# Hybrid decoder step: where the measures of the second and third units' weights stand at the start

## The chip, the cores and the metric

The kernel runs on one core of a Trainium2 chip. The metric is the time of one execution on the device in microseconds (us). The engines are named as the profile names them: PE is TensorE (matmuls; PEld its weight loads), DVE is VectorE, ACT is ScalarE, POOL is GpSimd, SP is SyncE, whose queue issues most DMAs.

## What is computed

One inference step of a decoder with two layers, for a prompt of 2048 tokens and 8 sample sequences of 4 new tokens (32 rows). Layer 0 is a linear attention (HGRN2) and a forgetting softmax attention side by side, behind one input projection; layer 1 is a gated linear attention (GLA).

```python
def even_mixer(h, w_in, ...):           # layer 0, h = rmsnorm(x, norm_even)
    proj = h @ w_in                     # 1024 -> 4*512 + 4*512 + 4
    qa, fa, ia, ga, qb, kb, vb, gb, fb = _split(proj, ...)
    f = lb + (1.0 - lb) * sigmoid(fa)
    o_a, s_a = gated_linear_chunked(qa, 1 - f, ia, log(f), hgrn_s0)
    o_a = head_rmsnorm(o_a, hgrn_gain) * silu(ga)
    o_b = fox_attend(qb, kb, vb, log_sigmoid(fb + b_fox)) * silu(gb)
    return concatenate([o_a, o_b]) @ w_out, ...
```

The change lies in the first 80 us of layer 0: the norm of the first 1056 token rows and the first columns of `h @ w_in`.

## The kernel before, in words

A full-precision product is made of three 16-bit ones: each operand is split into a high part (16 bit) and a low part (what is left), and a product is high x high, high x low, low x high (`mm3`, lines 467 to 469). Before a weight block is split it is scaled by a power of two. The scale comes from a **measure** (the largest absolute value: four reductions on VectorE, line 292, one for each quarter of the block, and one over the four results, line 294), a product on TensorE that spreads it over the partitions (`spr_...`, line 279) and a few tiny steps on VectorE (`pow_...`, lines 281, 270, 271, 272, 302; the reciprocal in line 272 is the scale). Then the **split**: of the four quarters, two go ScalarE L348 (scale), ScalarE L349 (high part), GpSimd L350 (low part), the other two ScalarE L345 (high part) and VectorE L346 (low part).

The input projection is cut into **units** of 256 weight columns. A unit has four steps: 0 fetch (DMAs), 1 measure, 2 scale, 3 split, and then its matmuls. The units of the first half of the tokens come in the order v0, g0, qf0, qf1, Bq0, Bg0, ...; in the program's names v0's weights are `Ai`, g0's `Ag`, those of qf0 and qf1 both `Aqf`. The raw weights are `wr_...`, the split ones `w_...`, the maxima `rm_...`. v0's outputs are `pt_Av` (four pairs of 128-token tiles, 48 matmuls each) and `pS_Av` (the 32 sample rows, from `sam_Av`, a copy of their columns; the four partial sums are added in line 516 and copied to `vs` in line 807). g0's are `pf_Ag`, in three segments of 352 columns of tokens for each of two halves; each ends in a silu (lines 523 to 525).

The tokens themselves are loaded (`nx`), normalized (lines 418, 400, 402, 420), turned by TensorE in pairs of 128-token tiles (`nt`, line 431), and split into `act`: high parts on ScalarE (line 462), low parts on VectorE (line 463). The last group is the 32 sample rows. The buffers of `nt` come free with the low parts. `self.last_v` is the latest low part written down so far.

`staged` runs the units: while unit j's matmuls are written down tile by tile, it writes down steps of the next units; the list `todo` says which, as pairs (unit, step), one list behind each tile. A scheduler then sets the order in each engine's queue; each engine works through its own queue strictly in that order. `issue_after(x)` binds all instructions in its block to stand behind x. The small constants of the kernel (`more_consts`: gains, `lb`, `wgr` and `wg`, masks `mlev` by way of `mtmp`, the cleared `scT`) are bound in this way behind the last token load, the last high part and the last low part.

Of the kernel before, what the change touches and what calls it, by code (L numbers as in the profile page):

```python
# [121 lines left out]
class Kern:  # L122
# [918 lines left out]
    def staged(self, us, a, b, beside=None):  # L1041

        def step(u, n):
            if u < len(us):
                self.ready[u] = us[u][0][n]()

        for j in range(a, b):
            if j:  # L1050
                todo = [[(j + 3, 0), (j + 2, 1)], [(j + 2, 2)], [(j + 2, 3)]]
            elif beside is None:
                todo = [[(2, 0), (1, 3)], [(3, 0)], [(2, 3)]]
            else:
                todo = [[(1, 0)], [], [(2, 0)], [(1, 1), (1, 2)], [(1, 3), (3, 0), (2, 1), (2, 2), (2, 3)]]
            for n, c in enumerate(us[j][1](self.ready.pop(j))):
                for x in todo.pop(0) if todo else ():
                    step(*x)
                if beside and n in (1, 3):
                    beside(2 * j + n // 2)  # L1060
                yield c
            for t in todo:
                for x in t:
                    step(*x)
# [896 lines left out]
```

## Time and profile before

| | before |
|---|---|
| timed runs (3) | 2403.77, 2410.35, 2413.72 us; median 2410.35 |
| profiled execution | 2408.25 us, its span 2405.8 us |
| mean granted clock of TensorE | 0.987 |
| PE busy | 2296.7 us (95%) |
| DVE, ACT, POOL busy | 1418.9, 1111.1, 744.1 us (59, 46, 31%) |
| DMA | 317.25 MB, mean 132 GB/s |

The span is what the trace covers; the execution's own time is 2.45 us longer. Times in rows count from the start of the span. A granted clock of 1.00 is TensorE's higher level (2.4 GHz), 0.50 the lower one (1.2 GHz). Matmuls are pipelined: each row shows some 0.27 us for a matmul of 256 columns, while they start 0.11 us apart at the higher clock.

### The profile page before, as it was taken

Reading aid. Unit: us, or ns where it says so; the run is one execution under the profiler, and the core shown is the slowest. Engines: PE = TensorE matmul, PEld = TensorE weight load, DVE = VectorE, ACT = ScalarE, POOL = GpSimd, SP = SyncE. Lnnn points to the kernel's source line nnn. Section 1 sums busy time; section 2 is a strip of 40 time slices with the busy share of each in tenths; the row PEclk is TensorE's granted clock in tenths of the full one; section 3 lists DMA queues with packets and bytes.
Section 4 is the critical chain, followed back from the end, with each engine's and each line's share of the span. In section 5 each row is a group of like instructions: output and inputs, shape, how many; then the busy total and the mean of one; then the engine's idle time right before and its main releaser. Section 6 shows DMA issues by size and latency. Waiting matters only on the chain. (4 is left out here: it accounts for less than half of the span.)

```text
span 2405.8 us, 58659 instructions
## 1 busy us (share of the span) xinstructions
PE 2296.7 (95%) x23324; PEld 1635.3 (68%) x23324; DVE 1418.9 (59%) x3345; ACT 1111.1 (46%) x2466; POOL 744.1 (31%) x839
## 2 busy tenths in 40 slices
PE   7999999999999999999997999999999999999998
PEld 5667668854655876655445876777678766666887
DVE  7556556546764548567667363665675644557554
ACT  6434243342433127466668254535443645545333
POOL 2233223112212225144465111432452222322222
PEclk9999999999999999999999999999999999999999
DMA  6231235435431276776865532122146312114453
GB/s 181 78 87 58 85 121 160 144 108 149 144 116 59 82 223 220 259 246 208 265 195 181 163 108 59 45 76 89 50 147 194 114 37 73 43 58 159 152 190 148
DMA packets 297013, 317.25 MB, mean 132 GB/s; under 512 B 39729, under 2 KB 241010, under 8 KB 296738
## 3 DMA queue, kind: packets, MB, share of 16 engines
q1 hardware_dynamic: 295234, 308.98, 40.7%
q8 instruction: 183, 3.00, 0.5%
q0 software_dynamic: 1504, 4.52, 0.5%
q14 instruction: 92, 0.75, 0.1%
HBM read 242.31 MB, written 71.11 MB: 130 GB/s over the span
## 5 line engine op out<-in xcount | busy, mean ns | idle before, releaser
L469 PE MATMUL pt_o<-w_o,act 128*128 128x256 f16 x1024 | 281.2, 275 | 4.1 <-DVE act L1597 3.9
L467 PE MATMUL pt_o<-w_o,act 128*128 128x256 f16 x1024 | 281.5, 275 | 2.4 <-ACT sg1C L523 2.4
L468 PE MATMUL pt_o<-w_o,act 128*128 128x256 f16 x1024 | 281.2, 275 | 0.0
L467 PEld LDWEIGHTS <-act 128*128 128x128 f16 x2304 | 226.9, 98 | 37.0 <-ACT act L462 4.7
L469 PEld LDWEIGHTS <-act 128*128 128x128 f16 x2304 | 226.8, 98 | 35.2 <-DVE act L1597 5.1
L468 PEld LDWEIGHTS <-act 128*128 128x128 f16 x2304 | 227.0, 99 | 33.6 <-issue 3.7
L467 PE MATMUL pt_Cv<-w_Cv,act 128*128 128x256 f16 (+1 forms) x512 | 140.3, 275 | 1.7 <-ACT act L462 0.9
L468 PE MATMUL pt_Cv<-w_Cv,act 128*128 128x256 f16 (+1 forms) x512 | 140.0, 274 | 0.0
L469 PE MATMUL pt_Cv<-w_Cv,act 128*128 128x256 f16 (+1 forms) x512 | 139.7, 274 | 0.0
L633 POOL TENSOR_TENSOR kA<-kA,fA 128x512 f32<-128x512 f32 (+1 forms) x56 | 79.0, 1411 | 191.6 <-PE gl_A L599 141.3
L1208 ACT ACTIVATE L<-L,nm,kc 128x512 f32<-128x512 f32 (+3 forms) x160 | 118.2, 740 | 37.9 <-DVE nm L1206 33.7
L633 POOL TENSOR_TENSOR kC<-kC,fC 128x512 f32<-128x512 f32 (+1 forms) x56 | 82.0, 1465 | 151.9 <-PE gl_C L599 112.5
L1216 POOL TENSOR_SCALAR L<-L,nm 128x512 f32<-128x512 f32 (+3 forms) x160 | 98.5, 629 | 65.3 <-DVE nm L1212 24.1
L1243 ACT ACTIVATE th<-pt 128x512 f16<-128x512 f32 (+3 forms) x159 | 80.6, 526 | 61.0 <-PE pt L1236 60.2
L1244 DVE TENSOR_TENSOR tl<-pt,th 128x512 f16<-128x512 f32 (+3 forms) x159 | 94.8, 609 | 22.1 <-ACT th L1243 21.0
L1236 PE MATMUL pt<-ident,L 128*128 128x128 f32 x544 | 91.9, 280 | 6.3 <-POOL L L1216 3.2
L1236 PEld LDWEIGHTS pt<-ident,L 128*128 128x128 f32 x544 | 67.2, 144 | 35.7 <-DVE tl L1244 8.7
L1360 PEld LDWEIGHTS pkt<-ident,pgcache_fox_k 128*128 128x128 f32 x512 | 57.5, 141 | 42.6 <-issue 25.1
L1360 PE MATMUL pkt<-ident,pgcache_fox_k 128*128 128x128 f32 x512 | 74.7, 278 | 7.3 <-DVE kts L1364 5.2
L467 PE MATMUL pt_Av<-w_Ai,act 128*128 128x256 f16 x256 | 70.5, 276 | 2.5 <-ACT act L462 2.5
L467 PE MATMUL fo<-th,h_v 128*128 128x512 f16 (+3 forms) x174 | 59.4, 341 | 12.4 <-ACT th L1243 9.5
L468 PE MATMUL pt_Av<-w_Ai,act 128*128 128x256 f16 x256 | 70.4, 275 | 0.8 <-POOL w_Ai L350 0.8
(950 smaller groups left out, 6756.6 us busy)
## 6 DMA issues: line engine op xcount, KB each, us to landing
pgcache_fox_k<-in_cache_fox_k SPq DMA_DIRECT2D x128, 256.0 KB, 4.3
pgcache_fox_v<-in_cache_fox_v SPq DMA_DIRECT2D x128, 256.0 KB, 3.9
yr<-yT SPq DMA_DIRECT2D x16, 1024.0 KB, 6.1
nx<-in_x_prompt SPq DMA_DIRECT2D x16, 512.0 KB, 4.9
wr_Aqf<-in_w_in_even SPq DMA_DIRECT2D x64, 128.0 KB, 3.8
wr_o<-in_w_out_even SPq DMA_DIRECT2D x32, 256.0 KB, 4.5
wr_Cv<-in_w_in_odd SPq DMA_DIRECT2D x32, 256.0 KB, 3.9
wr_Cqk<-in_w_in_odd SPq DMA_DIRECT2D x64, 128.0 KB, 3.0
```

The lines of the kernel that those rows point to most:

```text
L467: nc.tensor.matmul(ps, lh[0], rh[0], start=first, stop=False)
L468: nc.tensor.matmul(ps, lh[0], rh[1], start=False, stop=False)
L469: return nc.tensor.matmul(ps, lh[1], rh[0], start=False, stop=last)
L633: nc.gpsimd.tensor_tensor(kv[:, :, 0], kv[:, :, 0], t1.to_broadcast([P, nb, w]), ALU.mult)
L1208: self.last_exp = nc.scalar.activation(lt[:, :w], lt[:, :w], AF.Exp, bias=nm[:, 0:1], scale=ib, accum_out=nm[:, 2 + j : 3 + j])
L1216: nc.gpsimd.tensor_scalar(lt[:, :w], lt[:, :w], nm[:, 1:2], 2.0**14, ALU.mult, ALU.mult)
L1236: nc.tensor.transpose(pt[:, w : w + P], rows[b][s // 4][0][:, (s % 4) * P : (s % 4 + 1) * P], self.ident)
L1243: nc.scalar.activation(th[:, a:w], pt[:, a:w], AF.Copy),
L1244: nc.vector.tensor_tensor(tl[:, a:w], pt[:, a:w], th[:, a:w], ALU.subtract)))
L1360: nc.tensor.transpose(pk[:, j * P : (j + 1) * P], pgs[j][:, h * P : (h + 1) * P], self.ident)
```

## The change

```diff
         def step(u, n):
             if u < len(us):
-                self.ready[u] = us[u][0][n]()
+                with ExitStack() as st:
+                    if beside and n == 1 and u < 3:
+
+                        st.enter_context(self.tc.issue_after(self.last_v.ins))
+                    self.ready[u] = us[u][0][n]()
...
-                todo = [[(1, 0)], [], [(2, 0)], [(1, 1), (1, 2)], [(1, 3), (3, 0), (2, 1), (2, 2), (2, 3)]]
+                todo = [[(1, 0)], [], [(2, 0)], [(1, 1), (1, 2), (1, 3)], [(3, 0), (2, 1), (2, 2), (2, 3)]]
```

The measures of units 1 (g0, `Ag`) and 2 (qf0, the first `Aqf`) are bound behind the latest low part. When they are written down, in the lists behind v0's fourth pair of tiles and behind its sample rows, that is the last one of the sample rows. And g0's split is written down one place earlier, behind v0's last pair of full tiles, not behind the sample rows. No instruction is added or taken away.

What it does to VectorE's queue while the first token pairs are split (the difference; `act<-nt_5_229` is the low part of the sixth of eight row blocks of the first token pair, `nt_0_264` belongs to the second pair):

```order
 L346 SCALAR_TENSOR_TENSOR w_Ai_153<-wr_Ai_134,kc,w_Ai_153 128x2x256 x2
-L292 TENSOR_REDUCE rm_Ag_648<-wr_Ag_359 128x1
 L463 SCALAR_TENSOR_TENSOR act<-nt_5_229,g_even,act 128x256
-L292 TENSOR_REDUCE rm_Ag_648<-wr_Ag_359 128x1
 L400 TENSOR_SCALAR rst_n_189<-nss_187 128x1
-L292 TENSOR_REDUCE rm_Ag_648<-wr_Ag_359 128x1
 L463 SCALAR_TENSOR_TENSOR act<-nt_6_234,g_even,act 128x256
-L292 TENSOR_REDUCE rm_Ag_648<-wr_Ag_359 128x1
+L420 TENSOR_SCALAR nx_512_184<-nx_512_184,rsr_n_191 128x1024
 L463 SCALAR_TENSOR_TENSOR act<-nt_7_239,g_even,act 128x256
-L292 TENSOR_REDUCE rm_Aqf_717<-wr_Aqf_556 128x1
 L463 SCALAR_TENSOR_TENSOR act<-nt_0_264,g_even,act 128x256
```

The four measures of Ag and the four of the first Aqf (the other three stand a few rows on) are gone from among the low parts, and the norm of a later token tile (L420) has moved up.

VectorE's queue of the change from the last low part on (`nt_7_593` is the last row block of the sample rows):

```order
L463 SCALAR_TENSOR_TENSOR act<-nt_7_593,g_even,act 128x32
L292 TENSOR_REDUCE rm_Ag_648<-wr_Ag_359 128x1 x4
L506 COPY sam_Av_673<-act 128x8x32 x2
L292 TENSOR_REDUCE rm_Aqf_717<-wr_Aqf_556 128x1 x4
L165 TENSOR_SCALAR g_hgrn<-g_hgrn 128x4
L165 TENSOR_SCALAR g_gla<-g_gla 128x8
L172 TENSOR_TENSOR lb<-lb 128x4
L191 MEMSET wgr 80x512
L213 CAST mdiag<-ident 128x128
L232 MEMSET scT_835 128x1024
L232 MEMSET scT_836 128x1024
L294 TENSOR_REDUCE rm_Ag_648<-rm_Ag_648 128x1
```

The measures now stand here, among the constants, and the sum over Ag's four (L294) stands behind the two memsets of scT. Six short rows follow (a mask cast, the sum for Aqf, two gains, two of lb), then L196 (wg), L177 (lb), and these, on to the reciprocal that gives Ag's scale (the first L272):

```order
L281 TENSOR_REDUCE pow_Ag_656<-spr_Ag_654 128x1
L292 TENSOR_REDUCE rm_Aqf_883<-wr_Aqf_708 128x1 x4
L178 RECIPROCAL lb<-lb 128x4
L270 TENSOR_SCALAR pow_Ag_656<-pow_Ag_656 128x1
L210 CAST mlev_789<-mtmp 128x64
L210 CAST mlev_795<-mtmp 128x64
L516 TENSOR_TENSOR few_Av_701<-few_Av_701,pS_Av_676 32x256
L281 TENSOR_REDUCE pow_Aqf_725<-spr_Aqf_723 128x1
L294 TENSOR_REDUCE rm_Aqf_883<-rm_Aqf_883 128x1
L179 TENSOR_TENSOR lb<-lb 128x4
L271 TENSOR_SCALAR kc<-pow_Ag_656 128x1
L516 TENSOR_TENSOR few_Av_701<-few_Av_701,pS_Av_676 32x256
```

Behind these come L270 for Aqf, L184 (lb) and the L272. Before, the steps L281 to L302 of Ag stood among the low parts of the sample rows, around the measures of the second Aqf (`rm_Aqf_883`, whose place behind L281 of Ag is kept).

TensorE's queue of the change at the end of v0 (`nt_7_593` is the last transposition of the sample rows):

```order
L467 MATMUL pt_Av_597<-w_Ai_153,act 128x256
L431 MATMUL nt_7_593<-ident,nx_1024_364 128x32
L468 LDWEIGHTS act
L468 MATMUL pt_Av_597<-w_Ai_153,act 128x256
L469 LDWEIGHTS act
L469 MATMUL pt_Av_597<-w_Ai_153,act 128x256
L279 MATMUL spr_Ag_654<-ident,rm_Ag_648 128x128
L511 LDWEIGHTS sam_Av_673
L511 MATMUL pS_Av_676<-w_Ai_153,sam_Av_673 32x256
```

The product for Ag's scale (`spr_Ag`) now stands behind v0's last full-tile matmul and ahead of the sample rows' `pS_Av`; before, it stood between the first and the second transposition of the sample rows, well ahead of v0's end, and the last three transpositions stood behind v0's last matmul. Behind `pS_Av` stand `spr_Aqf_723`, four matmuls of `pf_Ag`, the product for the second Aqf (`spr_Aqf_918`, which before came one segment later), and then `pf_Ag` on. ScalarE has, behind v0's results, L195 (wg), the exponentials of lb, L514 (the sample sum), four steps of Ag's split (L348, L345, L348, L345), two copies to `vs` (L807) and the first L349 of Ag; before, Ag's split stood right behind v0's results and L807 behind all of it. In the attention phase some instructions stand in a slightly other order at about a dozen places.

## Rows read from the trace of the kernel before

**Rows 1.** The page: busy time, share of the span, instructions of each engine.

```profile
PE 2296.7 (95%) x23324; PEld 1635.3 (68%) x23324; DVE 1418.9 (59%) x3345; ACT 1111.1 (46%) x2466; POOL 744.1 (31%) x839
```

**Rows 2.** Table of stretches: busy us of each engine, granted clock, DMA share.

```profile
core 0: us, PE busy (x) PEld busy (x) DVE busy (x) ACT busy (x) POOL busy (x), PEclk, DMA share, GB/s
25.00:50.00 25.00, 25.00 (x224) 21.97 (x222) 18.30 (x49) 14.93 (x36) 4.27 (x7) 1.00 0.51 112
50.00:56.50 6.50, 2.65 (x37) 1.43 (x35) 5.18 (x20) 5.60 (x13) 1.59 (x2) 0.91 0.07 16
56.50:62.00 5.50, 5.50 (x20) 2.81 (x20) 5.13 (x16) 1.31 (x6) 3.30 (x10) 0.50 0.41 119
62.00:140.00 78.00, 77.08 (x886) 51.11 (x885) 46.87 (x107) 28.26 (x55) 24.30 (x27) 1.00 0.26 75
900.00:1300.00 400.00, 373.78 (x2628) 216.31 (x2627) 280.12 (x867) 259.77 (x585) 185.24 (x290) 0.98 0.67 219
```

**Rows 3.** Timeline of VectorE, first and last of eight measures (start, duration).

```profile
18.65 0.68 DVE L292 TENSOR_REDUCE rm_Ag<-wr_Ag 128x1 f32<-128x512 f32 x1
...
25.60 0.68 DVE L292 TENSOR_REDUCE rm_Aqf<-wr_Aqf 128x1 f32<-128x512 f32 x1
```

**Rows 4.** Timeline of TensorE; in brackets the wait before, and its releaser.

```profile
21.51 0.37 PE L468 MATMUL pt_Av<-w_Ai,act 128*128 128x256 f16 x1 [0.83 <-POOL w_Ai L350]
...
50.20 0.27 PE L469 MATMUL pt_Av<-w_Ai,act 128*128 128x256 f16 x1
50.40 0.37 PE L431 MATMUL nt<-ident,nx 32*128 32x32 f32 x3
...
54.89 0.32 PE L467 MATMUL pf_Ag<-act,w_Ag 128*128 128x352 f16 x1 [1.53 <-ACT w_Ag L349]
...
56.47 0.45 PE L467 MATMUL pf_Ag<-act,w_Ag 128*128 128x352 f16 x1 [1.11 <-DVE pow_Aqf L281]
```

**Rows 5.** Timeline of VectorE, 45 to 61 us.

```profile
46.21 2.46 DVE L292 TENSOR_REDUCE rm_Aqf<-wr_Aqf 128x1 f32<-128x512 f32 x4
...
49.82 0.16 DVE L272 RECIPROCAL kc<-kc 128x1 f32<-128x1 f32 x1
...
51.19 0.61 DVE L463 SCALAR_TENSOR_TENSOR act<-nt,g_even,act 128x32 f16<-128x32 f32 x3 [0.91 <-ACT act L462]
51.72 0.22 DVE L506 COPY sam_Av<-act 128x256 f16<-128x256 f16 x1
51.85 0.16 DVE L165 TENSOR_SCALAR g_hgrn<-g_hgrn 128x4 f32<-128x4 f32 x1
...
52.34 0.48 DVE L191 MEMSET wgr<- 80x512 f32 x1
...
54.13 0.91 DVE L232 MEMSET scT<- 128x1024 f32 x1 [0.16 <-issue]
...
54.98 1.10 DVE L174 TENSOR_TENSOR lb<-lb 128x4 f32<-128x4 f32 x1
...
59.03 0.68 DVE L196 TENSOR_TENSOR wg<-wgr,wg 16x512 fp32r<-16x512 f32 x1
...
59.94 0.42 DVE L516 TENSOR_TENSOR few_Av<-few_Av,pS_Av 32x256 f32<-32x256 f32 x1
```

**Rows 6.** Timeline of ScalarE, 50 to 62 us.

```profile
51.74 0.74 ACT L348 ACTIVATE wr_Ag<-wr_Ag,kc 128x512 f32<-128x512 f32 x1
...
54.19 0.64 ACT L349 ACTIVATE w_Ag<-wr_Ag 128x512 f16<-128x512 f32 x1
...
55.98 0.63 ACT L195 ACTIVATE wg<-wgr 80x512 fp32r<-80x512 f32 x1 [0.39 <-DMA wgr<-in_w_gla_gate]
...
60.99 0.69 ACT L807 ACTIVATE vs<-few_Av,kc 32x128 f32<-32x128 f32 x2 [4.19 <-DVE few_Av L516]
```

**Rows 7.** Timeline of GpSimd: the low parts of Ag.

```profile
54.91 2.26 POOL L350 TENSOR_TENSOR w_Ag<-wr_Ag,w_Ag 128x512 f16<-128x512 f32 x2 [20.31 <-ACT w_Ag L349]
```

**Rows 8.** Waits of TensorE, longest sum: us in total, times, longest us.

```profile
PE fo L467 <- ACT th L1243: 9.5, 7, 2.6
```

**Rows 9.** The page: DMA issues, count, KB each, median us from issue to landing.

```profile
wr_Aqf<-in_w_in_even SPq DMA_DIRECT2D x64, 128.0 KB, 3.8
```

## The prediction

> **What bounds the kernel now.** I read the page first: TensorE is busy for 2296.7 of 2405.8 us, 95% [rows 1]. So a microsecond counts only where TensorE stands still or runs at its lower clock, and one lost there is lost for good unless a later wait swallows it. Then the table of stretches [rows 2]: from 25 to 50 us, the first unit (v0), TensorE shows 25.00 of 25.00; from 62 to 140 us 77.08 of 78.00; between them lies the hole that this change moves. From 50 to 56.5 us it is busy 2.65 of 6.5, and from 56.5 to 62 us it works without a gap but at a granted clock of 0.50, the lower of its two levels (1.2 against 2.4 GHz).
>
> The rows around the hole [rows 4]: v0's last full-tile matmul starts at 50.20, three transpositions for the 32 sample tokens follow at 50.40, the second unit (g0, pf_Ag) begins at 54.89 after 1.53 us of waiting for ScalarE's w_Ag, and goes on for good from 56.47. The wait is for the split of g0's weights, which ScalarE starts at 51.74, as soon as v0's results are out; the first 16-bit part is done by 54.83 [rows 6]. It can start then because the scale was known early: its reciprocal ran at 49.82 on VectorE [rows 5]. The measures behind it had run far earlier, from 18.65 to 26.28: eight reductions of 0.68 us for Ag and the first Aqf, among the low parts [rows 3].
>
> **The change, part by part.** *At the front*, eight reductions (5.4 us) and their two sums leave VectorE's queue between 18.65 and 28 us; the low parts behind them come earlier. Who waits for those? TensorE's 0.83 us before 21.51 is put down to GpSimd's w_Ai, which the change leaves alone [rows 4], and from 25 us on there is no idle time to give back [rows 2]. In the new order TensorE also meets one more pair of transpositions (nt_3) before its run of v0 matmuls, whose buffer comes free with a low part of the second token pair. I bound the gain from 1 us (the 0.83 us and a little) to nothing and take nothing: v0's last matmul stays at about 50.2. If the cover of 25 to 50 us were gone, up to 5.4 us would be to be had; TensorE's full rows say that it isn't.
>
> *At the back* the eight reductions come behind the last low part, and in the new VectorE order the reciprocal that gives Ag's scale is the last of 44 instructions behind it. I count from the end of the last low part. Three of them stood at 51.19 to 51.80 [rows 5], 1.4 us after their three transpositions began [rows 4]. In the new order the last transposition stands two matmuls before v0's end; for one of the three I take 0.8 us, so the count begins near 50.8. Then, each from rows 5:
> - measures of Ag, four in 2.46 us, 2.4 to the next one's start; two sample copies of 0.22, 0.4; measures of Aqf, 2.4. Together 5.2.
> - the constants from L165 to the second scT memset: 51.85 to 55.04, less a sample copy that lies between (0.22 and its handover): 2.9. Now 8.1.
> - seven short ones (sums, a cast, gains, lb) at about 0.12 apart (their rows are some 0.15 long and overlap): 0.85. Now 8.95.
> - L196 needs ScalarE's L195, and that a DMA that goes out only when the memset of wgr is done. Before, that memset ended at 52.82 and L195 started at 55.98 for 0.63 us [rows 6], 3.16 us on. Now the memset ends at about 5.9, so L196 starts at 9.75, not 8.95: 0.8 of waiting, with all of VectorE's queue behind it. L196 takes 0.7: 10.45.
> - the third set of measures (the second Aqf, four reductions), which stands ahead of Ag's scale: 2.4, so 12.85.
> - two L516 additions at 0.4, and thirteen short ones at 0.12, the last of them the reciprocal: 15.2.
>
> So the scale is there at about 66.0, not at 49.98. ScalarE then needs four steps of the split (51.74 to 54.19, 2.45 us), the two vs copies that now stand between (0.69 together, 0.6 to the next start) and the first L349 (0.64) [rows 6]: with 0.1 us of handover 69.8. The first pf_Ag matmul falls at 69.85, where it was at 54.89: 15.0 us later. Two corrections. Before, TensorE stopped again for 1.11 us before 56.47 [rows 4]; now the low part from GpSimd (1.13 us, half of 2.26 [rows 7]) is ready after the first four matmuls at the lower clock (20 in 5.5 us [rows 2], 0.28 each), so 1.1 us comes back. And the small product for the second Aqf's scale now stands right there at the lower clock, some 0.4 us. Sum: 15.0 - 1.1 + 0.4 = **14.3 us later**.
>
> The clock costs the same on both sides: g0's first 5.5 us ran at 0.50 before, behind a hole of some 4 us, and will again behind a longer one. ScalarE's split traced earlier brings nothing, since it waits for the scale. Of DMAs none is added; the wr_Bq and wr_Bg loads wait for buffers that the split frees, so they move with it, and their units are the fifth and sixth, two and more units behind g0 (v0 took 25 us and more [rows 2]), which covers them.
>
> The bounds: the front's gain takes off up to 1 us; the short ones at 0.07 instead of 0.12 another 1.0; a slower wgr DMA or a fuller queue adds 1 to 2. So 12.3 to 16.3 from the steps. Further, the scheduler has put instructions of the attention phase in a slightly other order at about a dozen places, with the same work; the largest wait of TensorE there is 2.6 us long [rows 8], so I allow 4 us either way, and nothing as the likeliest.
>
> A rule that speaks against the change: VectorE's L174, on two tiny operands, took 1.10 us at 54.98, while GpSimd ran its two w_Ag steps from 54.91 to 57.17 [rows 5, 7]. The Trainium skill, "SBUF — State Buffer", section "Who interferes with whom", says that a VectorE instruction with two SBUF inputs and a GpSimd one that reads SBUF hold a shared port pair against each other for a whole instruction; the row agrees, 56.08 being just where the first half of GpSimd's work ends. By this rule GpSimd's mask selects, which now run beside L177 and L179, could hold them for up to some 1.9 us, and the sum would be about 16.2; by the rows alone it is 14.3.
>
> **The rivals.** *The delay is swallowed* (not slower): the attention phase from 900 to 1300 us has TensorE idle for 26.2 of 400 us, at a DMA share of 0.67 [rows 2]. If those waits are for page loads that don't start later when TensorE is late, they shrink by the delay. For it: the DMA share. Against: the waits of TensorE there are named as ScalarE's and VectorE's results [rows 8], which themselves follow TensorE's. It decides as soon as more than 2.2 us are swallowed (then the rest is under 0.5%, 12.05 us); all of it gives 2410.4, no change.
>
> *VectorE's relief at the front pays* (faster): if TensorE's rows from 20 to 25 us are late through low parts rather than GpSimd's weights, and the clock rises earlier, 5.4 us come off v0; that still leaves 14.3 - 5.4 = 8.9, 2419.3, within 0.5%. To be faster, Ag's scale would also have to be ready before v0's end, which the order of the queue excludes, so little is left for it.
>
> *A second stall behind the first* (slower still): in the new order two measures of wr_Bg stand ahead of the first silu step of g0 on VectorE. If that load lands after TensorE's third g0 segment is done, ScalarE and then TensorE's output buffers stop for it. It goes out when the first Aqf's split is through, near 76.5 by the same steps; such loads land 3.8 us on [rows 9], so its first two pieces are measured by 82. The third segment ends near 83 (72 matmuls from 69.85: 20 in 5.5 us, 52 at half of 0.28). The slack is 1 us; a landing of 5 to 7 us, or a longer split, makes it a stall of 1 to 4: 2426 to 2429.
>
> **How the numbers follow.** The profiled execution took 2408.25 us (span 2405.8), the three timed runs 2403.77 to 2413.72 with the median 2410.35, 2.1 above it. On the profiled one the sum gives 2422.6; against the median, which the result will be compared with, 2410.35 + 14.3 = **2424.7**, 0.59% slower. Chances: the forecast 0.64 (2418 to 2430), swallowed in part or whole 0.2, the second stall 0.11, the front's relief 0.05. About 0.5% is what a measurement of this kernel can tell from no change. The forecast lies only 2.2 us beyond that, so some of it falls within: slower 0.62, same 0.33, faster 0.05. The range 2412 to 2433 leaves out the runs in which nearly all is swallowed, and the second stall at its worst.
>
> **What would show it.** Right: VectorE's measures of Ag behind 50 us; TensorE idle from about 50 to 59, then again until about 70, with pf_Ag starting between 68 and 72; the granted clock at 0.50 for some 5 us behind it; TensorE full again thereafter, and the same work from 100 us on shifted by 12 to 16 us up to the end. Wrong: pf_Ag before 60 (the reciprocal came early), v0 over before 48 (the front pays), or a shift at 140 us that is smaller at 1400 us (swallowed).

## The result, and the profile after

| | before | after |
|---|---|---|
| timed runs | 14, median 2404.14 us (2398.41 to 2413.72) | 14, median 2415.93 us (2409.39 to 2419.33) |
| profiled execution, its span | 2408.25, 2405.8 us | 2416.09, 2414.2 us |
| mean granted clock | 0.987 | 0.986 |

The changed kernel is slower: its runs stand to those of before as 1.0046, with a 95% interval of 1.0036 to 1.0055, which is 11 us (9 to 13) and within the 0.5% that I had called no change. The forecast was 14.3 us more than before. Of the 8.8 us by which the time is under the 2424.7 of the forecast, 6.2 are the yardstick: the first three runs of before had a median of 2410.35, all fourteen 2404.14.

The page first, busy time of each engine as in [rows 1]:

```profile
PE 2293.2 (95%) x23324; PEld 1633.9 (68%) x23324; DVE 1418.6 (59%) x3345; ACT 1111.6 (46%) x2466; POOL 745.8 (31%) x839
```

Same work, same shares: the loss is in waiting. The table of stretches, to be set against [rows 2]:

```profile
25.00:50.00 25.00, 25.00 (x214) 21.66 (x212) 12.17 (x30) 14.07 (x34) 3.51 (x6) 1.00 0.51 111
50.00:56.50 6.50, 2.69 (x19) 1.36 (x16) 4.53 (x12) 1.99 (x6) 0.00 (x0) 0.87 0.00 0
56.50:62.00 5.50, 0.96 (x10) 0.68 (x14) 4.54 (x17) 0.00 (x0) 0.72 (x3) 0.50 0.10 19
62.00:70.00 8.00, 1.96 (x26) 1.09 (x18) 7.12 (x34) 3.08 (x8) 3.45 (x16) 0.50 0.00 1
70.00:76.00 6.00, 4.17 (x17) 2.54 (x18) 3.59 (x10) 6.00 (x13) 2.34 (x3) 0.56 0.30 87
76.00:140.00 64.00, 63.72 (x666) 41.79 (x663) 35.12 (x71) 22.56 (x41) 14.30 (x12) 1.00 0.22 67
```

From 53 to 72 us TensorE (first pair of numbers) does next to nothing, while VectorE (third pair) is busy. From 76 us on TensorE is full again; no second stall follows. TensorE's timeline around the hole, the answer to [rows 4] (start, duration, in brackets the wait and its releaser):

```profile
52.42 0.27 PE L469 MATMUL pt_Av<-w_Ai,act 128*128 128x256 f16 x1
...
61.04 0.80 PE L279 MATMUL spr_Ag<-ident,rm_Ag 128*128 128x128 f32 x2 [8.35 <-DVE rm_Ag L294]
...
71.83 0.47 PE L467 MATMUL pf_Ag<-act,w_Ag 128*128 128x352 f16 x1 [7.87 <-ACT w_Ag L349]
...
72.98 0.63 PE L279 MATMUL spr_Aqf<-ident,rm_Aqf 128*128 128x128 f32 x2
73.40 0.50 PE L469 MATMUL pf_Ag<-act,w_Ag 128*128 128x352 f16 x1
```

Two waits, 8.35 us for the sum over Ag's measures and 7.87 us for the split. VectorE's timeline shows what stood in front of them (compare [rows 5]):

```profile
52.72 0.25 DVE L463 SCALAR_TENSOR_TENSOR act<-nt,g_even,act 128x32 f16<-128x32 f32 x1 [0.25 <-ACT act L462]
52.89 2.45 DVE L292 TENSOR_REDUCE rm_Ag<-wr_Ag 128x1 f32<-128x512 f32 x4
...
55.52 2.46 DVE L292 TENSOR_REDUCE rm_Aqf<-wr_Aqf 128x1 f32<-128x512 f32 x4
57.90 0.17 DVE L165 TENSOR_SCALAR g_hgrn<-g_hgrn 128x4 f32<-128x4 f32 x1
...
60.88 0.10 DVE L294 TENSOR_REDUCE rm_Ag<-rm_Ag 128x1 f32<-128x4 f32 x1
...
61.26 0.15 DVE L174 TENSOR_TENSOR lb<-lb 128x4 f32<-128x4 f32 x1
62.69 0.68 DVE L196 TENSOR_TENSOR wg<-wgr,wg 16x512 fp32r<-16x512 f32 x1 [1.27 <-ACT wg L195]
...
63.68 2.45 DVE L292 TENSOR_REDUCE rm_Aqf<-wr_Aqf 128x1 f32<-128x512 f32 x4
...
67.94 0.14 DVE L272 RECIPROCAL kc<-kc 128x1 f32<-128x1 f32 x1
```

and ScalarE's (compare [rows 6]) the split that follows it at once:

```profile
68.11 0.72 ACT L348 ACTIVATE wr_Ag<-wr_Ag,kc 128x512 f32<-128x512 f32 x1 [4.45 <-DVE kc L272]
...
71.16 0.61 ACT L349 ACTIVATE w_Ag<-wr_Ag 128x512 f16<-128x512 f32 x1
```

To see how far the delay travels, one takes the same product in both traces. Here the spread products for a later Bg and for the output weights, in the timelines of TensorE before:

```profile
276.91 0.39 PE L279 MATMUL spr_Bg<-ident,rm_Bg 128*128 128x128 f32 x2
...
512.36 0.39 PE L279 MATMUL spr_o<-ident,rm_o 128*128 128x128 f32 x2
```

and after:

```profile
291.46 0.38 PE L279 MATMUL spr_Bg<-ident,rm_Bg 128*128 128x128 f32 x2
...
522.60 0.38 PE L279 MATMUL spr_o<-ident,rm_o 128*128 128x128 f32 x2
```

So 14.6 us at 277 us, 10.2 at 512, and 8.4 at the end of the spans (2414.2 less 2405.8). Two things were not forecast: v0's last matmul starts at 52.42, not 50.20, and some of the delay seems to come back.

### The profile page after: what moved, and what is told of

The parts are those of the page before. It is cut to its first block, busy times and chain, and to the rows that moved or that the text cites. A ratio compares the mean times of both kernels' runs of the same rounds, so it can differ in the third digit from the quotient of the medians.

```text
span 2414.2 us, 58658 instructions
## 1 busy us (share of the span) xinstructions
PE 2293.2 (95%) x23324; PEld 1633.9 (68%) x23324; DVE 1418.6 (59%) x3345; ACT 1111.6 (46%) x2466; POOL 745.8 (31%) x839
```

## The experiments

Three theories had to be tested. *Place in the queue*: what costs is where the rows of Ag's scale stand in VectorE's queue. *Lock*: v0 lost 2.2 us at the front because a VectorE instruction and GpSimd's hold each other up. *Swallowed* against *passed on*: does the kernel have slack behind 300 us, or do the executions differ in low-clock stretches that come or don't?

**Each half of the change alone.** `todo_only` keeps the new list and takes the binding out:

```diff
-                    if beside and n == 1 and u < 3:
+                    if beside and n == 1 and u < 0:
```

`bind_only` keeps the binding and has the old list:

```diff
-                todo = [[(1, 0)], [], [(2, 0)], [(1, 1), (1, 2), (1, 3)], [(3, 0), (2, 1), (2, 2), (2, 3)]]
+                todo = [[(1, 0)], [], [(2, 0)], [(1, 1), (1, 2)], [(1, 3), (3, 0), (2, 1), (2, 2), (2, 3)]]
```

In the orders that the scheduler makes, `todo_only` is row for row the kernel before on all engines, and `bind_only` the changed kernel; so is a kernel that binds Ag's measures alone (not run). The whole change is thus the binding of four measures.

> Only the second half of the change (g0's split written down one place earlier), no binding. The scheduler puts every engine's queue in the same order as before, row for row. Expected: ratio 1.000, within 0.1%. The profile is a second look at the kernel before. Theory 'chance of the clock' (part of the delay was given back in the profile because three low-clock stretches of before, at 362.6, 809.7 and 1724.5 us, did not come in the changed kernel): this second look also lacks some of these or has others. Rival 'slack' (the kernel gives the delay back systematically at fixed places): all stretches of before come again at the same places.

> Only the first half of the change (the measures bound behind the last low part), with the old list of steps. Every engine's queue is in the same order as in the changed kernel. Expected: as the changed kernel, ratio to before 1.0046 (1.0036 to 1.0055), some 11 us. The profile is a second look at the changed kernel: v0's last matmul at 52.4, the first pf_Ag at 71.8. By 'slack' its shift against before falls from 14.6 us at 300 us to some 9 to 11 at the same places as in the first look; by 'chance of the clock' it falls, or not, at other places.

Measured: 1.0007 (0.9993 to 1.0021) and 1.0057 (1.0039 to 1.0075). In `bind_only` v0's last matmul starts at 51.84 and pf_Ag at 71.23, both 0.6 us earlier than in the changed kernel. The order of before again had its low clock at 362 us, and the changed order again had none there; it was 13.6 us late at 277 us and 8.8 at 512. That suggested a place where delay is always swallowed; what follows takes this apart.

**The front.** `front_order` binds the normalization of the third token pair behind the first pair's last low part, and leaves the back alone:

```diff
-            if t < len(groups):
+            if t < len(groups) and not (late and t == LAG_N):
                 groups[t][0]()
             if 0 <= t - LAG_N < len(groups):
                 groups[t - LAG_N][1]()
+                if late and t == LAG_N:
+                    with late(): groups[t][0]()
```

(`late` is `issue_after(self.last_v.ins)`.)

> The changed kernel, but the normalization of the third token tile pair (L420, the one that took 1.75 us beside GpSimd's w_Ai) is bound behind the last low part of the first pair; the back is left alone. Theory 'lock' (L420 was held by GpSimd's w_Ai, and with it the first pair's last low parts, and so TensorE): TensorE's run of v0 starts 1 us or more earlier than 22.68, the last matmul of v0 at 50.5 (49.5 to 51.2) in place of 52.42, the total some 2 us under the changed kernel, ratio to before 1.0038. Rival 'order' (TensorE lost it because one more pair of transpositions stands ahead of the run): v0's end stays at 52.4, ratio 1.0046.

The timelines of VectorE, GpSimd and TensorE in the changed kernel:

```profile
19.99 1.75 DVE L420 TENSOR_SCALAR nx<-nx,rsr_n 128x1024 f32<-128x1024 f32 x1
...
20.04 2.72 POOL L350 TENSOR_TENSOR w_Ai<-wr_Ai,w_Ai 128x512 f16<-128x512 f32 x2
...
22.19 0.69 PE L431 MATMUL nt<-ident,nx 128*128 128x128 f32 x2 [1.38 <-DVE act L463]
22.68 0.42 PE L468 MATMUL pt_Av<-w_Ai,act 128*128 128x256 f16 x1
```

and in `front_order`:

```profile
23.40 0.74 DVE L420 TENSOR_SCALAR nx<-nx,rsr_n 128x1024 f32<-128x1024 f32 x1
...
20.39 2.27 POOL L350 TENSOR_TENSOR w_Ai<-wr_Ai,w_Ai 128x512 f16<-128x512 f32 x2 [4.10 <-ACT w_Ai L349]
...
20.53 1.41 PE L431 MATMUL nt<-ident,nx 128*128 128x128 f32 x4
21.74 0.42 PE L468 MATMUL pt_Av<-w_Ai,act 128*128 128x256 f16 x1
...
50.47 0.27 PE L469 MATMUL pt_Av<-w_Ai,act 128*128 128x256 f16 x1
```

The L420 that took 1.75 us takes 0.74 away from GpSimd's pair, that pair 2.27 in place of 2.72, TensorE's wait is gone, and v0's last matmul starts at 50.47: the theory of the lock holds, and the one more pair of transpositions costs 0.3 us at most.

The wait of 1.38 us is not the whole of the 2.2. It makes v0's run of matmuls start 0.8 us later than before; the rest comes behind it, with TensorE busy all the time. The table of stretches, two of before and then two of the changed kernel:

```profile
24.00:26.00 2.00, 2.00 (x18) 1.68 (x16) 2.00 (x6) 0.75 (x3) 0.55 (x1) 1.00 1.13 365
26.00:28.00 2.00, 2.00 (x21) 1.85 (x19) 2.00 (x7) 0.47 (x1) 0.92 (x1) 1.00 1.14 263
```

```profile
24.00:26.00 2.00, 2.00 (x11) 1.56 (x10) 1.27 (x5) 0.43 (x2) 0.55 (x1) 1.00 1.12 364
26.00:28.00 2.00, 2.00 (x13) 1.49 (x12) 0.88 (x2) 0.47 (x1) 0.00 (x0) 1.00 1.20 249
```

The table counts 39 matmuls in these 4 us before and 24 in the changed kernel, at the same full busy time and the same granted clock of 1.00: they start 0.21 us apart until about 27.5 us, before only until 24.7, and 0.11 us apart from then on. In `front_order` it is 39 again. Why the closer spacing comes later is not shown beyond that.

The total of `front_order` did not follow (1.0062, 1.0046 to 1.0077): its profile had low clocks at 304 and 376 us. The same kernel a second time, `front_order_b`:

> The same kernel as front_order, a second look. If the place of a low-clock stretch follows from the kernel and its delay, those at 304.4 and 376.1 us, which neither before nor the changed kernel has, come again; if it is chance from run to run, at least one of them is missing. Total: ratio 1.004 to 1.006.

v0's last matmul at 50.12; the low clock at 304 us was missing, the one at 376 came again; 1.0035 (1.0022 to 1.0048), a little under the expected range. So the same kernel has such a stretch in one execution and not in another.

**The back.** `consts_late` puts the constants behind Ag's scale:

```diff
-        nc.vector.reciprocal(out[:, 0:1], out[:, 1:2])
+        self.last_r = nc.vector.reciprocal(out[:, 0:1], out[:, 1:2])
...
-                            tc.issue_after(self.last_v.ins):
+                            tc.issue_after(self.last_v.ins), tc.issue_after(self.last_r.ins):
```

> The changed kernel, but all constants stand behind the reciprocal that gives Ag's scale; the measures still stand behind the last low part. Theory 'queue' (what counts is the number of rows between the last low part and the reciprocal): two sets of measures 4.9, sample copies 0.3, sums and the product for the scale 1.1, the third set 2.4, some ten short rows and two L516 1.6: reciprocal 10.3 us behind the last low part instead of 15.2, first pf_Ag near 66.9 in place of 71.8, ratio to before 1.0025, about 5 us under the changed kernel. Rival 'swallowed' (the length of the hole does not reach the end): 1.0046 still. Rival 'next in the queue' (the late constants stop something else, as wg or lb): a new wait of TensorE above 1 us between 75 and 140.

Its first pf_Ag, from TensorE's timeline, and at the front L420 and GpSimd's pair:

```profile
66.14 0.47 PE L467 MATMUL pf_Ag<-act,w_Ag 128*128 128x352 f16 x1 [6.47 <-ACT w_Ag L349]
...
20.16 0.75 DVE L420 TENSOR_SCALAR nx<-nx,rsr_n 128x1024 f32<-128x1024 f32 x1
...
20.21 2.83 POOL L350 TENSOR_TENSOR w_Ai<-wr_Ai,w_Ai 128x512 f16<-128x512 f32 x2
```

The reciprocal came 10.1 us behind the first measure (51.54 to 61.64), 10.3 were expected, and the work at 277 us stood 9.0 us late, not 14.6. Here L420 started the same 0.05 us ahead of GpSimd as in the changed kernel and kept its 0.75 us, and GpSimd was held instead (2.83); v0's last matmul came at 51.07, still 0.9 us later than before (13 matmuls from 24 to 26 us, where before has 18). In the total nothing of this was seen: 1.0058 (1.0044 to 1.0072). The same kernel a second time:

> The same kernel as consts_late, a second look: is its total really no better than the changed kernel's, though its work from 100 to 300 us stands 5.6 us earlier? 'Passed on': the mean of the runs comes to 9 us or so above before over both looks, ratio about 1.004; if it stays at 1.0055 or more, the low-clock stretches later in the program take back what was won, and this look should show more of them than the changed kernel's (mean clock 0.985 or less).

9.7 us late at 277 us, and again 1.0051 (1.0035 to 1.0067), at a mean clock of 0.985 over 13 runs. What is won before 100 us is there in both traces and not in the timed runs. The two executions do show what happens between 277 and 512 us. The table of stretches from 355 to 400 us, for the first and then the second:

```profile
355.00:400.00 45.00, 42.51 (x712) 33.98 (x711) 31.83 (x69) 16.64 (x36) 19.51 (x15) 1.00 0.42 129
```

```profile
355.00:400.00 45.00, 42.07 (x655) 32.92 (x654) 30.70 (x73) 15.72 (x33) 17.72 (x14) 0.92 0.35 111
```

The same kernel, once at clock 1.00 and once with a low stretch (0.92). At 512 us the first is 4.0 us behind before and the second 10.0. Two of TensorE's products show where they drift apart, in the first:

```profile
377.33 0.66 PE L915 MATMUL BkT<-ident,Bk 128*128 128x128 f32 x4 [0.61 <-DVE Bk L890]
426.31 0.60 PE L571 MATMUL py_A<-ident,on_A 128*128 128x128 f32 x4
```

and in the second:

```profile
381.46 0.66 PE L915 MATMUL BkT<-ident,Bk 128*128 128x128 f32 x4
432.25 0.63 PE L571 MATMUL py_A<-ident,on_A 128*128 128x128 f32 x4 [1.64 <-DVE on_A L564]
```

They are 0.7 us apart at 277 us, 4.1 behind the low stretch and 5.9 behind py_A, where only the second waits for VectorE. Before's profile has both, the low stretch (0.92) and a wait at py_A (0.84 us at 420.83); the changed kernel's has neither. So much of the "give-back" is a low stretch, and a wait behind it, that one execution has and the other has not.

`ag_early` lifts the binding from Ag alone, so that Ag is measured early, as before:

```diff
-                    if beside and n == 1 and u < 3:
+                    if beside and n == 1 and u == 2:
```

> The changed kernel without the binding for Ag: Ag's four measures are among the first low parts as before, only the first Aqf's stay behind the last low part. In its VectorE queue the later steps of Ag's scale still stand behind the constants and a set of Aqf measures. Theory 'place of the scale' (what counts is where the reciprocal stands in the queue, not when Ag was measured): reciprocal some 9.5 us behind the last low part, first pf_Ag 4 to 7 us earlier than 71.8, ratio to before 1.002 to 1.003. Rival 'measures' (2.45 us of Ag's measures behind the last low part are the cost): pf_Ag back at 55 to 57, ratio 1.000 to 1.001.

VectorE's timeline:

```profile
52.80 0.28 DVE L281 TENSOR_REDUCE pow_Ag<-spr_Ag 128x1 f32<-128x128 f32 x1
...
58.90 0.14 DVE L270 TENSOR_SCALAR pow_Ag<-pow_Ag 128x1 f32<-128x1 f32 x1
...
61.83 0.16 DVE L272 RECIPROCAL kc<-kc 128x1 f32<-128x1 f32 x1
```

The product for the scale is back at 52.80, and the next tiny step, which needs nothing else, starts 6.1 us later: constants and Aqf's measures stand between. First pf_Ag at 65.73, 1.0019 (1.0008 to 1.0030). The measures of Ag are the smaller part of the cost: with them early again, pf_Ag is still 10.8 of the 16.9 us later than before. The larger part is the place of the steps behind them. The reciprocal came 11.2 us behind the last low part, 9.5 were expected: a second set of measures stood there, which I had counted once.

`both` joins the two repairs:

> The changed kernel with both repairs, the normalization behind the first pair's last low part and the constants behind Ag's scale. If the two costs add: v0's last matmul at 50.5, first pf_Ag 14.8 to 15.3 us behind it as in the kernel with the constants late, so at 65.3 to 65.8; the work from 100 to 300 us 7.5 to 9 us later than before. 'Passed on': ratio 1.003 to 1.005; 'swallowed': under 1.002.

v0's last matmul at 50.82, pf_Ag at 65.79, 8.7 us late at 277 us, 1.0030 (1.0014 to 1.0046): here the gain does show in the total.

**A delay and nothing else.** `hold` is the kernel before with TensorE held up between v0 and g0:

```diff
+                if hf == 0:
+                    ps = pps.tile([P, 512], F32, tag="pj", name="hold")
+                    with tc.issue_after(self.last_a.ins):
+                        for _ in range(160):
+                            nc.tensor.matmul(ps[:, :P], self.ident, self.ident, start=True, stop=True)
+                    nc.vector.tensor_copy(self.few.tile([P, 1], F32, tag="hold", name="hc"), ps[:, :1])
                 drain(dense(1, 3))
```

> The kernel before with 160 products of the identity with itself (their result goes nowhere) between v0's sample product and g0, which hold TensorE busy: a delay and nothing else. They start some 0.11 us apart at the higher clock, 17.6 us, of which about 5 lie in the hole that was there, and the hole's low-clock stretch (6.8 us at half, some 2.8 us lost) does not come: the work from 100 to 300 us is 9 to 12 us later. Theory 'passed on' (on average nothing is swallowed later, what differs at the end is low-clock stretches that come or don't): mean of the timed runs 8 to 13 us above before, ratio 1.0035 to 1.0055, and the low-clock stretch near 362 us (plus the delay) again or not. Rival 'swallowed' (the kernel has slack behind 300 us): 4 us or less, ratio under 1.002.

A 32-bit product is two matmuls in the trace, so the 160 took 36 us, twice what I had allowed: the work was 30.7 us late at 277 us. The total is 1.0149 (1.0128 to 1.0170), 31 to 41 us. All of it arrives, and some 5 us more that are not explained; a delay as such is not swallowed.

**A version that beats both.** `split_early` takes the kernel before, without any binding, and writes Ag's steps down earlier:

```diff
-                todo = [[(1, 0)], [], [(2, 0)], [(1, 1), (1, 2)], [(1, 3), (3, 0), (2, 1), (2, 2), (2, 3)]]
+                todo = [[(1, 0)], [(1, 1)], [(2, 0), (1, 2)], [(1, 3)], [(3, 0), (2, 1), (2, 2), (2, 3)]]
```

> The kernel before, with g0's three later steps written down one to two places earlier (measure behind the second tile pair, scale behind the third, split behind the fourth). The measures stay where they were; ScalarE's split of Ag now stands ahead of the last sample rows' high parts. Theory 'the hole is the price of a late split': first pf_Ag at 52 to 54 in place of 54.89, ratio to before 0.9990 to 0.9998. Rival: the split in ScalarE's queue delays the sample rows' high parts and so v0's end and the sample product, pf_Ag later than 55, ratio 1.000 to 1.001.

TensorE's timeline:

```profile
53.23 0.31 PE L467 MATMUL pf_Ag<-act,w_Ag 128*128 128x352 f16 x1
...
66.27 0.45 PE L467 MATMUL pf_Ag<-act,w_Ag 128*128 128x352 f16 x1 [3.25 <-DVE few_Av L516]
```

pf_Ag is 1.7 us earlier, as expected, and then a new wait of 3.25 us stands at 66.27, which the trace puts down to the additions of v0's sample rows (L516), with the low clock behind it (1.00 from 55 to 62 us, 0.52 from 65 to 72): 2.7 us late at 277 us, 1.0013 (1.0000 to 1.0026), where less than 1 was expected. `mid0` has the front of `front_order`, Ag's measures bound behind the second pair's low parts (the condition's last part is `u == 1`), and the list

```diff
+                todo = [[(1, 0), (1, 1)], [(1, 2)], [(2, 0), (1, 3)], [], [(3, 0), (2, 1), (2, 2), (2, 3)]]
```

`mid` has the list of `split_early`, with the same front and the binding behind the third pair.

> The front order of front_order, with Ag's measures bound behind the second token pair's last low part (so in the middle of v0, where VectorE has room), its scale and split written down one and two places earlier than in the kernel before. If the theories of the front and of the hole hold: no measures among the first low parts, v0's run from about 21.5 on, its end at 50 or earlier, w_Ag ready before v0 ends, first pf_Ag at 51 to 53 without waits above 0.5 us; ratio to before 0.9975 to 0.9990 (2 to 6 us). Rival 'swallowed' (what is gained before 60 us is lost at the first later wait): 0.9995 to 1.0005. Rival 'sample rows': their high parts come late behind the split, TensorE waits over 2 us for them.

> As mid0, but Ag's measures bound behind the third token pair's last low part, scale and split one place later. VectorE has less time between the measures and v0's end: the reciprocal stands among the sample rows' low parts. Expected: first pf_Ag at 53 to 55, ratio to before 0.998 to 1.000, 1 to 2 us above mid0. Rival: the measures stop the fourth pair's low parts and transpositions, v0's end later than 51, ratio above 1.000.

`mid0`, table of stretches:

```profile
50.00:62.00 12.00, 11.53 (x98) 7.57 (x99) 8.87 (x33) 4.31 (x13) 2.15 (x6) 1.00 0.34 98
```

The hole is closed and the clock stays at 1.00 in it; but a transposition at 41.92 waits 1.22 us for a step of Ag's scale; with that and more that is not taken apart here, v0's last matmul comes at 53.69 and pf_Ag at 55.09, not at 51 to 53. In `mid` they come at 51.79 and 54.89. `mid0` stands 2.6 us ahead of before at 277 us, `mid` 1.3. Both: 0.9985 (0.9972 to 0.9998, and 0.9971 to 0.9999), 3.6 us faster than before, by intervals that just leave out a ratio of 1, and some 15 faster than the change. Which of their parts does it was not separated.

All delays (by the spread product that stands at 276.91 before) beside the totals (what the ratio is over 1, times 2404.5 us, the mean of the 78 runs of before that were made beside the experiments):

| kernel (two values where it ran twice or two share a row) | late at 277 us | total | clock 355 to 400 us | late at 512 us |
|---|---|---|---|---|
| mid0, mid | -2.6, -1.3 | -3.6, -3.6 | 0.92, 1.00 | -4.9, -4.9 |
| todo_only | 0.3 | 1.7 | 0.92 | -0.3 |
| split_early | 2.7 | 3.1 | 0.92 | 0.9 |
| ag_early | 8.2 | 4.6 | 1.00 | 3.9 |
| both | 8.7 | 7.2 | 0.92 | 8.8 |
| consts_late, consts_late_b | 9.0, 9.7 | 13.9, 12.3 | 1.00, 0.92 | 4.0, 10.0 |
| front_order, front_order_b | 12.0, 13.3 | 14.9, 8.4 | 0.92, 0.92 | 12.5, 12.4 |
| after, bind_only | 14.6, 13.6 | 11.1, 13.7 | 1.00, 1.00 | 10.2, 8.8 |
| hold | 30.7 | 35.8 | 0.94 | 30.2 |

The totals lie between 4.9 us under and 5.1 over the delays, 0.05 over them in the mean of the thirteen. One by one they match less well: for after, ag_early, consts_late, front_order_b and hold the delay lies outside the 95% interval of the total, three times above it and twice below, and one and the same kernel gave 14.9 and 8.4. With the clock at 1.00 from 355 to 400 us, the work at 512 stands 3.6 to 5.0 us better than at 277; with the low stretch, from 2.3 better to 0.5 worse (in `hold` the stretch runs on past 400).

## Why the prediction was right, and where not

*The back* held to the tenth. From the first measure to the reciprocal's end I had summed 15.2 us; the rows give 52.89 to 68.08. Its terms: two sets of measures and the copies 5.2 (57.90 - 52.89 = 5.0), constants 2.9 (3.0), L196 9.75 us in, held by ScalarE's L195 (62.69: 9.8), the third set 2.4 (2.4). From the scale to pf_Ag 3.85 (3.75). The second wait of before did go away, and the product for Aqf cost 0.42. `consts_late` and `ag_early` show that it is the queue: with the constants taken out from between, or Ag measured early, the reciprocal started 5.0 and 4.0 us nearer to the last low part.

*The step that failed* is "v0's last matmul stays at about 50.2": it started 2.2 us later (1.6 in `bind_only`, the same order). The gain that I bounded there from 1 us to nothing was indeed nothing (50.47 and 50.12 in `front_order`, with the same eight measures gone); what I missed is that a queue relieved of work moves what is left onto something else, L420 onto GpSimd's split of w_Ai. I had also read "25.00 of 25.00" as a stage with nothing to lose; the changed kernel shows 25.00 of 25.00 from 25 to 50 us as well, with 214 matmuls in place of 224, so a full busy time does not show how close the matmuls stand. Both outcomes of the meeting were seen in one and the same kernel: VectorE held (L420 1.75 us in `consts_late_b`) or GpSimd held (2.83 for two in `consts_late`). This is the rule that I had weighed at the back, the Trainium skill, "SBUF — State Buffer", section "Who interferes with whom": VectorE and GpSimd share a port pair, which one of them holds for a whole instruction, and VectorE's `tensor_scalar` is among those that can take it. The rows at the front agree with it: L420 at 1.75 us in place of 0.75, and the pair of L350 at 2.72 in place of 2.27. At the back, where I had allowed 1.9 us for it, L179 took 0.15 us beside a mask select of GpSimd and L177 0.16 beside a memset: no hold there.

*"The clock costs the same on both sides"* was off by some 1.6 us to the other side: pf_Ag's start (+16.9), less the wait that went (1.1), plus the product (0.4), makes 16.2, and 14.6 arrive at 277 us. Before, g0 worked on at 0.50 past 62 us; now most of the low clock lies inside the wait, and g0 meets only the last of it (0.56 in the mean from 70 to 76). Its fifth matmul is 16.4 us late (57.01 and 73.40), its 23rd 14.8 (62.25 and 77.04); the last 0.2 go where the second Aqf's product stood before. So that the 14.6 matches the sum of 14.3 is luck: two errors of opposite sign, +2.2 and -1.6, stand in it.

*Swallowed*, my rival with 0.2, looked right in the first pair of profiles (14.6, 10.2, 8.4), by the sign that I had named for it. For a delay as such it is not: `hold` passes all of its 30.7 us on. What differs between executions is in good part whether a low-clock stretch comes at a stall, around 362 us above all. That some 3 us of the change's own 14.6 are lost on the way is not excluded by this. In the 78 runs of before the mean granted clock tells much of the spread: 22 runs at 0.990 took 2402.2 us in the mean, 14 at 0.987 2405.9, 4 at 0.985 2411.5.

*The front's relief* (0.05) paid nothing. *The second stall* did not come: TensorE shows 63.72 of 64 us behind 76. *The range* of 2412 to 2433 held the time. The narrower forecast of 2418 to 2430, to which I had given 0.64, did not: 2415.93 lies 2 us under it, which the yardstick alone (6.2) would make up. By my own line of 0.5%, what was measured is "no change", to which I had given 0.33.

Open stays why `consts_late` does not show its 5 us in 13 timed runs while `both`, with the same back, does; the mean clock of its runs (0.985 against 0.986) says where to look, not why. Open too is what makes the total of the change 11 us (bind_only, the same order, 13.7) and not 14.6: the meeting at the front, which can end either way, and the low-clock stretches are both at hand, but only profiled executions show them.

## What to carry to other kernels

Binding an instruction behind another puts it behind everything that the queue already holds there: count the rows between it and what it must release, constants and the waits among them, and find out which half of a change moves any row at all before pricing both. Work taken out of a queue moves what is behind it: look up what each moved row will then run beside. One pair of profiles shows where a delay arises, not how much of it survives; for that, put in a pure delay and compare several executions of each kernel. And a busy share of 100% does not say that nothing was lost: count the matmuls in the stretch.

## What was not expected of the hardware

An L420 of 0.75 us took 1.75 beside GpSimd's L350, and in the trace of before the one L420 of 1.53 us, at 294.62, also ran beside GpSimd work (L686); starts 0.05 us apart, VectorE first, ended either way. A low-clock stretch follows a stall in one execution and not in another of the same kernel: 0.92 and 1.00 from 355 to 400 us. The stall's length doesn't tell: before, TensorE waited 1.93 us ahead of the low clock at 362 us, at the same instruction in the changed kernel 2.41, and the clock stayed at 1.00.
